# Between the stages of an attention and feed-forward layer: natural token order, first products by column parts, w_out split by halves, evictions and down splits re-dealt

## The chip, the cores and the metric

The kernel runs on one core of a Trainium2 chip. A core has TensorE (PE: matmuls and transposes, with results in PSUM banks), VectorE (DVE), ScalarE (ACT), GpSimd (POOL) and SyncE (SP, which issues the DMAs here). The metric is the device time of one execution in microseconds (us). The granted clock is the share of TensorE's full speed (2.4 GHz) that the chip allowed; the lower of its two levels is 1.2 GHz.

## What is computed

One layer: x is (1024, 1024), float32. Dilated attention in three groups, an output projection w_out (512 to 1024) and a residual; then RMSNorm, an up projection to 2 x 2816, a causal convolution of width 3 over tokens, silu(gate) x up, a down projection and a residual.

```python
def dilated_attention_mixer(h, w_in, q_gain, k_gain, w_out):
    ...
    o = jnp.sum(weights[..., None] * jnp.stack(outs).astype(jnp.float32), axis=0)
    return o.astype(h.dtype).reshape(B, S, ATTN_GROUP_WIDTH) @ w_out

def conv_ffn(h, w_up, conv_w, conv_b, w_down):
    u = causal_depthwise_conv(h @ w_up, conv_w, conv_b)
    gate, up = jnp.split(u, 2, axis=-1)
    return (jax.nn.silu(gate) * up) @ w_down

    ...
        x = x + mix
        x = x + conv_ffn(rms_norm(x, ffn_norm[layer]), ...)
```

## The kernel before, in words

**Products.** A float32 product is three matmuls in fp32r on split operands: a high part h, a cast by ACT, and a low part l = raw - h, a subtract by DVE or POOL. `split` (L514) and `put` (L590) do such a split; the results lie in a ring of 12 buffers (`ring`).

**Stage 1**, to about 604 us, computes the attention in six units over eight token blocks. The last unit runs into what follows.

**Between the stages**, for each of eight token tiles of 128 tokens: `turn_o` (L536) transposes the attention output on PE into a bank otr and splits it (oT), `out_project` (L544) multiplies it with one column half of w_out in 12 matmuls of 512 columns (y) and adds the result to x1, `norm2` (L556) makes the normed tile xn, and `turn2` (L564) transposes that in two halves (xT), which ACT copies to h. The feed-forward products use seven products of quarter operands in place of eight (a Strassen-like scheme over even and odd token tiles and both halves of D): `even` (L594) splits an even tile into the operands b1, `odd` (L598), in three steps, makes the five sums and differences of an odd tile with its even neighbour and splits them into bt. Each pair of tiles fills 128 of the 512 columns of these operands. `split_wo` (L521) splits the four row blocks of w_out, 1024 columns each. The order of the tiles is 0, 1, 2, 3, 4, 6, 5, 7.

**Stage 2** goes over 22 pairs n of a gate and an up feature block. `Pair.first`, `second`, `third` and `fourth` split the weights (wx, wy, wz, wv), `sums` makes the sums that wy and wz are split from (sy, sz), `product(p)` (L664) runs 12 matmuls of 512 columns in the order p = 1, 2, 5, 6, 3, 7, 4 into the banks ua, ub and uc, `evict` (L684) empties a bank on ACT or DVE, and `conv`, `silu`, `gate` and `outer` make the gated rows and their sums, which go to memory.

**Stage 3**, the down projection, has 77 steps (7 products by 11 row blocks). `load_down`, `split_down` and `down` load, split and multiply one step: four token tiles, three matmuls each.

**What sets the order.** The four compute engines run their instructions in the order in which the program calls them. In stage 1 and between the stages that order comes from a list, `plan`: `at(t, f)` puts a call at time t, and the list is sorted by t (N is its length of stage 1, T at L35 has the offsets). From L881 on the calls stand in the order in which they run: the first three pairs by hand, then the loop from L945, then the down steps with LEAD = 2 (how many steps ahead a split stands) and AHEAD = 5 (a load).

```python
    for p, i in enumerate(order):
        t = N + T["t0"] + 6 * p
        at(t + T["to"] if i else t + T["to0"], turn_o, i)
        at(t, out_project, i, 0)
        at(t + 3, out_project, i, 1)
        at(t + 5.8, norm2, i)
```

Of the kernel before, what the change touches and what calls it, by code (L numbers as in the profile page):

```python
# [8 lines left out]
F32 = mybir.dt.float32  # L9
# [26 lines left out]
         sm=6.5, w0=8.3, ws0=9.35, w1=10.0, ws1=11.95, mw=10.0, a0=12.2, a1=13.3, mo=12.2,  # L36
         fin=14.4, t0=4, so0=1.2, so1=1.4, so2=3.2, so3=3.3, to0=-2.2, to=-3.6, n2=3.0, n2s=5.8,
         xf=-9.8, xs=-5.0, xt=-3.5, wp=1, bd=0.5, bh=0)
# [3 lines left out]
def trunk(ctx: ExitStack, tc: tile.TileContext, x, mixer_norm, ffn_norm, w_in, q_gain, k_gain,  # L42
# [477 lines left out]

    def split_wo(kt):  # L521
        M.wo[kt] = split(M.wo[kt], "wo", nc.gpsimd if kt == 1 else nc.vector)

# [12 lines left out]
    def turn_o(i):  # L536
        tr = PA.tile([P, 4, P], F32, name="otr", tag="vp", bufs=1)
        for j in range(4):
            nc.tensor.transpose(tr[:, j], M.ol[i][:, j * P:(j + 1) * P], ident)
        M.oT[i] = oT = ring("oT", [P, 2, 4, P])  # L540
        nc.scalar.copy(oT[:, 0], tr)
        nc.vector.tensor_sub(oT[:, 1], tr, oT[:, 0].bitcast(F32))

    def out_project(i, hf):  # L544
        y = PQ.tile([P, 512], F32, name="y", tag="qk", bufs=2)
        oT = M.oT[i]
        cs = slice(hf * 512, (hf + 1) * 512)
        for kt in range(4):
            wh, wl = M.wo[kt]
            nc.tensor.matmul(y, oT[:, 0, kt], wh[:, cs], start=kt == 0, stop=False)  # L550
            nc.tensor.matmul(y, oT[:, 0, kt], wl[:, cs], start=False, stop=False)
            nc.tensor.matmul(y, oT[:, 1, kt], wh[:, cs], start=False, stop=kt == 3)
        x1 = M.x1[i]
        nc.vector.tensor_add(x1[:, cs], x1[:, cs], y)
# [71 lines left out]
    class Pair:  # L626
# [11 lines left out]

        def first(self):
            self.X = split(self.raw[0], "wx", nc.gpsimd)  # L640

# [10 lines left out]

        def second(self):
            self.Y = split(self.sy, "wy", nc.gpsimd)

        def third(self):
            self.Z = split(self.sz, "wz", nc.gpsimd)

# [4 lines left out]

        def product(self, p):  # L664

# [4 lines left out]
                4: ("V", 0, ("bt", 1), "a", False)}[p]  # L670
            if begin:
                pool, tag, bufs = (M.PL, "b", 2) if bank == "b" or self.n == 0 and bank == "a" else (M.PR, bank, 3)
                self.acc[bank] = pool.tile([P, 512], F32, name="u" + bank, tag=tag, bufs=bufs)
            acc, w, a = self.acc[bank], getattr(self, W), getattr(M, b)
            for k in range(4):
                for n, (z, y) in enumerate(((0, 0), (0, 1), (1, 0))):
                    nc.tensor.matmul(acc, w[z][:, s + k], a[y][:, j, k], start=begin and k == 0 and n == 0,  # L677
                                     stop=k == 3 and n == 2, skip_group_check=True)
            self.evict(p)

# [71 lines left out]

    at(N + 1.05, second_phase)
    at(N + 1.06, make_b1)
    for kt in range(4):
        at(N - 12, load_wo, kt)
        at(N + T[f"so{kt}"], split_wo, kt)
    order = [0, 1, 2, 3, 4, 6, 5, 7]
    for p, i in enumerate(order):
        t = N + T["t0"] + 6 * p  # L760
        at(t - 8 if i < 2 else t - 7, load_o, i)
# [7 lines left out]
        for q in range(2):  # L769
            at(t + 9.2 + .1 * q, turn2, i, q)  # L770
        if i % 2 == 0:
            at(t + 12.2, even, i)
        elif i < 5:
# [106 lines left out]

    p0, p1, p2 = pairs[:3]  # L881
# [24 lines left out]
    p0.product(5)  # L906
    p0.fourth()
    p1.sums(0)
    p0.product(6)
    p1.second()  # L910
    p1.sums(1)
    p0.product(3)
    p0.conv(False)
    p1.third()
    p0.product(7)
    p0.silu()
# [73 lines left out]
    M.RR = M.rr.__enter__()  # L990
    AHEAD, LEAD, TAIL = 5, 2, 3
    acc = {}
    for n, (b, i) in enumerate([(b, i) for b in range(2) for i in range(4)]):
        pool, tag, bufs = (M.PL, "b", 2) if n < 2 else (M.PR, "ac"[n % 2], 3)
        acc[b, i] = pool.tile([P, 512], F32, name="y", tag=tag, bufs=bufs)
    load_down(3)
    load_down(4)
    for m, (p, k) in enumerate(steps):
# [48 lines left out]
```

## Time and profile before

| | |
|---|---|
| median of three runs | 1352.21 us (1351.98 to 1354.04) |
| the profiled execution | 1352.94 us, span 1351.0 us |
| granted clock, mean | 0.981 |
| busy PE / DVE / ACT / POOL | 96% / 67% / 46% / 37% |
| stretches with PE idle or at the lower clock | 603 to 622, 676 to 763, 1127 to 1145 us |

The span is what the profiler saw of the program; the execution's own time has 1.9 us more around it. Times in rows are from the span's start. In a timeline row stand the start, the duration, the engine, the line (L), the operation, out<-in by the program's names and, in brackets, the idle time of that engine before it and what ended it. A matmul's duration includes its drain, which the next one overlaps; the spacing of starts tells the rate.

### The profile page before, as it was taken

How to read it: one execution, taken by the hardware profiler on the slowest of the kernel's cores; microseconds unless marked ns; L12 is line 12 of the kernel's file. 1: busy time of each engine (PE TensorE's matmuls, PEld its weight loads, DVE VectorE, ACT ScalarE, POOL GpSimd, SP SyncE). 2: the span in 40 equal slices, each digit the busy share in tenths (PEclk: the TensorE clock that was granted, in tenths of full speed). 3: DMA queues.
4: the chain of work that ended last, by engine and by line, in shares of the span. 5: the costliest groups of instructions: out<-in, count | busy, mean ns of one | idle time of the engine just before them, and what ended most of it. 6: DMA issues, size and time to landing. Idle time of an engine off the chain costs nothing.

```text
span 1351.0 us, 19176 instructions
## 1 busy us (share of the span) xinstructions
PE 1295.4 (96%) x6887; PEld 1084.4 (80%) x6887; DVE 900.2 (67%) x1537; ACT 615.4 (46%) x1272; POOL 501.2 (37%) x601
## 2 busy tenths in 40 slices
PE   6999999999989999999978899999999998999998
PEld 4898887888878888877766688888888886888887
DVE  4665465554564665556666888888888888776665
ACT  4565354453463453343534445444445445434432
POOL 3333245332364555544544444454445442000000
PEclk9999998999999999997989999999999998999999
DMA  7112211111110211123621323323332328963341
GB/s 238 46 57 76 82 52 56 37 49 58 45 56 25 72 51 36 35 68 113 204 68 39 103 93 112 100 87 92 117 117 87 109 69 306 335 211 107 101 143 60
DMA packets 111613, 132.15 MB, mean 98 GB/s; under 512 B 6126, under 2 KB 80030, under 8 KB 111518
## 3 DMA queue, kind: packets, MB, share of 16 engines
q1 hardware_dynamic: 111518, 130.93, 30.3%
q8 instruction: 54, 0.88, 0.3%
q14 instruction: 41, 0.34, 0.1%
HBM read 95.91 MB, written 35.00 MB: 97 GB/s over the span
## 4 chain that ended last, share of the span: by engine, by line
PE 45%; DVE 3%; POOL 1%; issue 1%; ACT 1%; DMA 0%; DVEq 0%; POOLq 0%; ACTq 0%
PE ua L677 17%; PE y L851 16%; PE uc L677 8%; PE ub L677 4%; DVE c L717 1%; POOL bt L592 0%; DMA graw<-gde 0%; ACT c L715 0%; DVE xn L561 0%; DVE c L728 0%; DVE sy L646 0%; POOL b L592 0%; PE xT L571 0%; ACT xn L559 0%; DVE sz L650 0%
## 5 line engine op out<-in xcount | busy, mean ns | idle before, releaser
L851 PE MATMUL y<-wd,g 128*128 128x512 f32 x924 | 213.3, 393 | 2.7 <-DVE g L592 1.2
L851 PEld LDWEIGHTS y<-wd,g 128*128 128x128 f32 x924 | 175.4, 190 | 40.5 <-DVE g L592 1.5
L198 PE MATMUL qk<-w,hh 128*128 128x512 f32 x384 | 159.4, 415 | 0.0
L199 PE MATMUL qk<-w,hh 128*128 128x512 f32 x384 | 153.8, 401 | 0.0
L200 PE MATMUL qk<-w,hl 128*128 128x512 f32 x384 | 152.6, 397 | 0.5 <-DVE hl L116 0.5
L79 POOL TENSOR_SCALAR ms<-ss 128x8 f32<-128x8 f32 (+1 forms) x64 | 12.8, 201 | 316.2 <-DVE ss L216 265.4
L207 PE MATMUL vp<-w,hh 128*128 128x256 f32 x384 | 122.8, 320 | 3.2 <-DVE v L228 3.1
L717 DVE SCALAR_TENSOR_TENSOR c<-uu,cw,c 128x1023 f32<-128x1023 f32 (+1 forms) x44 | 96.4, 2190 | 39.9 <-ACT c L715 39.2
L209 PE MATMUL vp<-w,hl 128*128 128x256 f32 x384 | 108.8, 283 | 0.0
L208 PE MATMUL vp<-w,hh 128*128 128x256 f32 x384 | 108.8, 283 | 0.0
L518 POOL TENSOR_TENSOR wyl<-sy,wyh 128x1024 fp32r<-128x1024 f32 x22 | 57.9, 2632 | 120.4 <-ACT wyh L517 63.5
L80 POOL TENSOR_TENSOR rs<-ms,half 128x8 f32<-128x8 f32 (+1 forms) x64 | 87.5, 1367 | 5.4
L200 PEld LDWEIGHTS qk<-w,hl 128*128 128x128 f32 x384 | 73.4, 191 | 18.7 <-DVE hl L116 1.2
L207 PEld LDWEIGHTS vp<-w,hh 128*128 128x128 f32 x384 | 73.6, 192 | 18.4 <-DVE v L228 5.6
L314 ACT ACTIVATE sm<-sm,ust 128x128 f32<-128x128 f32 (+1 forms) x128 | 53.3, 418 | 76.0 <-DVE ust L311 73.4
L267 ACT ACTIVATE qT<-tr,gains 128x256 fp32r<-128x256 f32 x48 | 22.7, 473 | 137.8 <-PE tr L256 137.8
L216 DVE TENSOR_REDUCE ss<-qn 128x8 f32<-128x512 f32 x48 | 32.9, 685 | 75.3 <-ACT qn L214 75.3
L208 PEld LDWEIGHTS vp<-w,hh 128*128 128x128 f32 x384 | 73.6, 192 | 9.3
L270 DVE SCALAR_TENSOR_TENSOR qT<-tr,gains,qT 128x256 fp32r<-128x256 f32 x48 | 23.2, 484 | 86.7 <-ACT kT L269 86.7
L198 PEld LDWEIGHTS qk<-w,hh 128*128 128x128 f32 x384 | 74.2, 193 | 0.5 <-ACT hh L115 0.4
L199 PEld LDWEIGHTS qk<-w,hh 128*128 128x128 f32 x384 | 74.3, 194 | 0.1
L311 DVE CUSTOM_DVE_ANT_0 sm<-s,mask 128x128 f32<-128x128 f32 (+1 forms) x192 | 56.1, 348 | 26.4 <-PE s L289 21.0
(182 smaller groups left out, 3374.5 us busy)
## 6 DMA issues: line engine op xcount, KB each, us to landing
uraw<-in_ffn_w_up SPq DMA_DIRECT2D x44, 512.0 KB
raw<-in_attn_w_in SPq DMA_DIRECT2D x48, 384.0 KB
wB<-in_ffn_w_down SPq DMA_DIRECT2D x44, 256.0 KB
graw<-gds SPq DMA_DIRECT2D x44, 256.0 KB
gdo<-c SPq DMA_DIRECT2D x11, 512.0 KB
gds<-gbc SPq DMA_DIRECT2D x11, 512.0 KB
graw<-gdo SPq DMA_DIRECT2D x22, 256.0 KB
ud<-ust SPq DMA_DIRECT2D x32, 132.0 KB
```

The lines of the kernel that those rows point to most:

```text
L80: nc.gpsimd.tensor_tensor(r[:, :n], t[:, :n], half[:, :n], op=ALU.pow)
L198: nc.tensor.matmul(self.qk, a, w[:, 0, :512], start=k == 0, stop=False)
L199: nc.tensor.matmul(self.qk, a, w[:, 1, :512], start=False, stop=False)
L200: nc.tensor.matmul(self.qk, b, w[:, 0, :512], start=False, stop=k == KT - 1)
L207: nc.tensor.matmul(self.vp, a, w[:, 0, 512:], start=k == 0, stop=False)
L208: nc.tensor.matmul(self.vp, a, w[:, 1, 512:], start=False, stop=False)
L209: nc.tensor.matmul(self.vp, b, w[:, 0, 512:], start=False, stop=k == KT - 1)
L311: nc.vector.tensor_tensor_reduce(out=sm[:, h, lo:], in0=src[h], in1=m, op0=ALU.add, op1=ALU.min, scale=-1.0, scalar=3e38, accum_out=st[:, ...
L518: eng.tensor_sub(l, raw, h.bitcast(F32))
L677: nc.tensor.matmul(acc, w[z][:, s + k], a[y][:, j, k], start=begin and k == 0 and n == 0, stop=k == 3 and n == 2, skip_group_check=True)
L717: nc.vector.scalar_tensor_tensor(c[:, k:], u[:, :S - k], cw[:, 2 - k, j:j + 1], c[:, k:], op0=ALU.mult, op1=ALU.add)
L851: nc.tensor.matmul(y, gs[:, z, ts], ws[:, w], start=f and n == 0, stop=k == NK - 1 and n == 2, skip_group_check=True)
```

## The change

1. w_out is split by column halves: `split_wo(kt, hf)` splits 512 columns at a time, the first halves of all four blocks first, the second halves later; `second_phase`, which opens the buffers, comes earlier. `turn_o(0)` comes earlier and uses a bank of tag "s" in place of "vp".
2. Tiles go in the order 0 to 7. Tile 6's operands are split by DVE straight from PSUM, and its copies to h (`turned`) come after that. The steps of `odd(5)` move into the list. Loads and first splits of pairs 0 and 1 come earlier.
3. Products 1 and 2 of pair 0 run on columns 0 to 383 before tile 7 is transposed and on columns 384 to 511 after it. `sum_bank` allocates pair 0's bank uc ahead of pair 1's first bank. wyl and wzl of pair 0 and two bt splits move from POOL to DVE. Sums, conv, gate and outer of pairs 1 to 3 stand at other places.
4. At the end of stage 2 the first three loads stand together, the splits of steps 0, 1 and 2 lie on POOL inside the last pair's products 6, 3 and 7, the first two groups of step 0's matmuls come ahead of the last product 4, and LEAD is 3.

```diff
-         fin=14.4, t0=4, so0=1.2, so1=1.4, so2=3.2, so3=3.3, to0=-2.2, to=-3.6, n2=3.0, n2s=5.8,
+         fin=14.4, t0=4, so=1.2, so0=3.2, so1=3.3, so2=5.1, so3=5.2, to0=-3.43, to=-3.6, n2=3.0, n2s=5.8,
...
-    def split_wo(kt):
-        M.wo[kt] = split(M.wo[kt], "wo", nc.gpsimd if kt == 1 else nc.vector)
+    def split_wo(kt, hf):
+        w = ring("wo", [P, 2, 512])
+        put([w[:, 0], w[:, 1]], M.wo[kt][:, hf * 512:(hf + 1) * 512], nc.gpsimd if kt == 1 else nc.vector)
+        M.wo[kt, hf] = w
...
     def turn_o(i):
-        tr = PA.tile([P, 4, P], F32, name="otr", tag="vp", bufs=1)
+        tag, bufs = ("vp", 1) if i else ("s", 2)
+        tr = PA.tile([P, 4, P], F32, name="otr", tag=tag, bufs=bufs)
...
-        if q == 0 or i % 2 == 0:
-            nc.scalar.copy(M.h[i][:, 4 * q:4 * q + 4], pt)
+        if i < 6 and i % 2 == 0 or i % 2 and q == 0:
+            turned(i, q)
...
     def even(i):
         c = slice(i // 2 * P, (i // 2 + 1) * P)
-        put([b[:, :, :, c] for b in M.b1], M.h[i].rearrange("p (a k) t -> p a k t", a=2), nc.gpsimd)
+        if i < 6:
+            put([b[:, :, :, c] for b in M.b1], M.h[i].rearrange("p (a k) t -> p a k t", a=2), nc.gpsimd)
+        else:
+            for q in range(2):
+                put([b[:, q, :, c] for b in M.b1], M.pt[i, q], nc.vector)
...
-    at(N + 1.05, second_phase)
+    at(N + .56, second_phase)
...
-        at(N + T[f"so{kt}"], split_wo, kt)
-    order = [0, 1, 2, 3, 4, 6, 5, 7]
-    for p, i in enumerate(order):
-        t = N + T["t0"] + 6 * p
+        at(N + T["so"] + .1 * kt, split_wo, kt, 0)
+        at(N + T[f"so{kt}"], split_wo, kt, 1)
+    for i in range(8):
+        t = N + T["t0"] + 6 * i
...
-    at(t - 10, pairs[0].load)
-    at(t - 3, pairs[0].first)
-    at(t + 3, pairs[1].load)
+    at(t - 12, pairs[0].load)
+    at(t - 7.5, pairs[0].first)
+    at(t - 4, pairs[1].load)
+    at(t + 3.1, pairs[1].first)
...
-    odd(5, 0)
-    p1.first()
-    p0.product(1)
-    p0.product(2)
+    p0.product(1, 0, 384)
+    p0.product(2, 0, 384)
     p2.load()
     for q in range(2):
         turn2(7, q)
-    odd(5, 1, nc.vector)
+    p0.product(1, 384)
     odd(7, 0)
+    p0.product(2, 384)
...
-    odd(5, 2, nc.gpsimd)
+    p0.sum_bank()
+    odd(7, 1, onV)
     p1.product(1)
+    odd(7, 2, onV)
     p2.first()
     p1.product(2)
     p0.sums(0)
-    p0.second()
-    odd(7, 1, nc.vector)
+    p0.second(onV)
     p2.product(1)
-    odd(7, 2, nc.gpsimd)
     p0.sums(1)
     p2.product(2)
-    p0.third()
+    p0.third(onV)
...
+        if p is None:
+            for m in range(8):
+                b, i = divmod(m, 4)
+                pool, tag, bufs = (M.PL, "b", 2) if m < 2 else (M.PR, "ac"[m % 2], 3)
+                if m == 2:
+                    down(0, 0)
+                    down(0, 1)
+                    old.product(4)
+                acc[b, i] = pool.tile([P, 512], F32, name="y", tag=tag, bufs=bufs)
+            old.conv(True)
+            old.gate()
+            break
         old.product(4)
         old.conv(True)
-        if p is None:
-            split_down(1, nc.gpsimd)
-            old.gate()
-            break
...
-            split_down(0, nc.gpsimd)
-            load_down(2)
+            split_down(0, onG)
         p.product(3)
...
+            split_down(1, onG)
         p.product(7)
+        if not new:
+            split_down(2, onG)
...
-    AHEAD, LEAD, TAIL = 5, 2, 3
+    AHEAD, LEAD, TAIL = 5, 3, 3
```

**ACT at the end of stage 1**, around the first splits of w_out (woh and wo are the high parts of w_out, oT the split attention output, v and pT belong to stage 1). Before:

```order
L214 ACTIVATE qn<-qk 128x512
L227 CAST v<-vp 128x4x64
L517 CAST woh<-wraw 128x1024
L328 CAST pT<-pt 128x512
L517 CAST woh<-wraw 128x1024
L541 CAST oT<-otr 128x512
L364 ACTIVATE e<-e 128x12
L517 CAST woh<-wraw 128x1024 x2
L328 CAST pT<-pt 128x512
```

Now:

```order
L214 ACTIVATE qn<-qk 128x512
L544 CAST oT<-otr 128x512
L227 CAST v<-vp 128x4x64
L597 CAST wo<-wraw 128x512 x2
L328 CAST pT<-pt 128x512
L597 CAST wo<-wraw 128x512 x2
L364 ACTIVATE e<-e 128x12
L597 CAST wo<-wraw 128x512 x2
L328 CAST pT<-pt 128x512
```

The cast of the first oT stands ahead of v, and the first halves of w_out are cast 512 columns at a time, two to a place, where one of 1024 stood.

**DVE at the start of stage 2** (h and bt are `odd`'s, ug the evictions of product 2, sy and sz the sums of the weights, wyl and wzl low parts of pair 0). Before:

```order
L692 TENSOR_TENSOR ug<-p_7697,ub 128x4x128
L592 TENSOR_TENSOR bt_7254<-h,bt_7253 128x8x128
L604 TENSOR_TENSOR h<-xT,h 128x512
L605 TENSOR_TENSOR h<-xT,h 128x512
L606 TENSOR_TENSOR h<-xT,h 128x512
L592 TENSOR_TENSOR bt_7254<-xT,bt_7253 128x4x128
L608 TENSOR_TENSOR h<-h 128x512
L692 TENSOR_TENSOR ug<-p_7757,ub 128x4x128
L646 TENSOR_TENSOR sy<-uraw 128x512
L647 TENSOR_TENSOR sy<-sy,uraw 128x512
```

Now:

```order
L598 TENSOR_TENSOR bt_7262<-xT,bt_7261 128x4x128
L618 TENSOR_TENSOR h<-h 128x512
L707 TENSOR_TENSOR ug<-p_7752,ub 128x4x128
L598 TENSOR_TENSOR bt_7262<-h,bt_7261 128x8x128 x2
L707 TENSOR_TENSOR ug<-p_7794,ub 128x4x128
L656 TENSOR_TENSOR sy<-uraw 128x512
L657 TENSOR_TENSOR sy<-sy,uraw 128x512
L518 TENSOR_TENSOR wyl<-sy,wyh 128x1024
L660 TENSOR_TENSOR sz<-uraw,sy 128x512
L661 TENSOR_TENSOR sz<-uraw 128x512
L707 TENSOR_TENSOR ug<-p_7837,ub 128x4x128
L518 TENSOR_TENSOR wzl<-sz,wzh 128x1024
```

Two splits into bt follow one another, and the splits wyl and wzl stand among the evictions and the sums; before, they were POOL's.

**ACT at the end of stage 2** (wd and g are a down step's operands, u and uu evictions of the last pair, c its conv and silu). Before:

```order
L591 CAST wv<-uraw 128x512
L698 COPY u_10697<-ua 128x512
L591 CAST wd<-wB_10657 128x512
L591 CAST g<-graw 128x512
L715 ACTIVATE c<-ug,cw 128x1024
L725 ACTIVATE c<-c 128x1024
L706 COPY uu<-ua 128x4x128
L715 ACTIVATE c<-uu,cw 128x1024
L591 CAST wd<-wB_10681 128x512
```

Now:

```order
L597 CAST wv<-uraw 128x512
L713 COPY u_10735<-ua 128x512
L597 CAST wd<-wB_10691 128x512
L597 CAST g<-graw 128x512
L597 CAST wd<-wB_10695 128x512
L597 CAST g<-graw 128x512
L597 CAST wd<-wB_10699 128x512
L597 CAST g<-graw 128x512
L730 ACTIVATE c<-ug,cw 128x1024
L740 ACTIVATE c<-c 128x1024
L721 COPY uu<-ua 128x4x128
L730 ACTIVATE c<-uu,cw 128x1024
```

Three steps are cast ahead of the conv of the gate half, where one was; the second step stood behind the conv of the up half.

## Rows read from the trace of the kernel before

**Rows 1.** The page, part 1: busy us (share of the span) and instructions of TensorE:

```profile
PE 1295.4 (96%) x6887; PEld 1084.4 (80%) x6887; DVE 900.2 (67%) x1537; ACT 615.4 (46%) x1272; POOL 501.2 (37%) x601
```

**Rows 2.** Windows view of three stretches; the line ahead of them names the columns:

```profile
core 0: us, PE busy (x) PEld busy (x) DVE busy (x) ACT busy (x) POOL busy (x), PEclk, DMA share, GB/s
603.00:622.00 19.00, 15.77 (x66) 11.56 (x65) 12.76 (x23) 8.81 (x18) 9.32 (x13) 0.64 0.29 103
676.00:763.00 87.00, 71.90 (x283) 54.98 (x283) 60.94 (x54) 34.34 (x43) 38.18 (x18) 0.92 0.20 61
1127.00:1145.00 18.00, 14.41 (x47) 10.50 (x46) 14.24 (x17) 10.19 (x18) 1.81 (x1) 0.81 1.00 361
```

**Rows 3.** Timeline of PE, 604 to 624 us: start, duration, instruction, idle before it:

```profile
605.52 0.66 PE L539 MATMUL otr<-ident,ol 128*128 128x128 f32 x4 [1.72 <-DVE v L228]
...
607.58 0.50 PE L550 MATMUL y<-woh,oT 128*128 128x512 f32 x1 [0.97 <-ACT oT L541]
...
612.08 0.80 PE L551 MATMUL y<-wol,oT 128*128 128x512 f32 x1 [0.53 <-DVE wol L518]
```

**Rows 4.** The same timeline: spacing of 512-column matmuls at both clock levels:

```profile
613.10 0.63 PE L550 MATMUL y<-woh,oT 128*128 128x512 f32 x1
613.53 0.68 PE L551 MATMUL y<-wol,oT 128*128 128x512 f32 x1
...
623.60 0.39 PE L550 MATMUL y<-woh,oT 128*128 128x512 f32 x1
623.82 0.39 PE L551 MATMUL y<-wol,oT 128*128 128x512 f32 x1
```

**Rows 5.** Groups by line of PE, 676 to 763 us: busy and mean, then idle before and its releasers:

```profile
L677 PE MATMUL ua<-b,wxh 128*128 128x512 f32 x32 | 13.1, 499 | 3.4 <-DVE h L604 3.4
L677 PE MATMUL ua<-bt,wv 128*128 128x512 f32 x36 | 10.6, 450 | 4.8 <-DVE uu L704 4.8
...
L677 PE MATMUL ua<-b,wxl 128*128 128x512 f32 x16 | 8.0, 500 | 1.9 <-POOL wxl L518 1.9
L677 PE MATMUL uc<-bt,wyh 128*128 128x512 f32 x24 | 7.8, 400 | 0.4 <-DVE bt L592 0.4
...
L677 PE MATMUL uc<-bt,wyl 128*128 128x512 f32 x12 | 5.0, 412 | 1.4 <-POOL wyl L518 1.4
L677 PE MATMUL uc<-bt,wzl 128*128 128x512 f32 x12 | 4.8, 404 | 0.9 <-POOL wzl L518 0.9
...
L571 PE MATMUL xT<-ident,xn 128*128 128x128 f32 x16 | 2.1, 276 | 2.4 <-DVE xn L561 2.4
```

**Rows 6.** Timelines of ACT and DVE, 604 to 616 us: splits of w_out:

```profile
604.58 1.04 ACT L517 CAST woh<-wraw 128x1024 fp32r<-128x1024 f32 x1
...
610.73 2.63 DVE L518 TENSOR_TENSOR wol<-wraw,woh 128x1024 fp32r<-128x1024 f32 x2 [0.61 <-ACT woh L517]
```

**Rows 7.** Timelines of DVE and POOL, 666 to 730 us: one instruction beside POOL and before it:

```profile
668.55 1.28 DVE L561 SCALAR_TENSOR_TENSOR xn<-x,rs,gbc 128x1024 f32<-128x1024 f32 x1 [2.17 <-POOL rs L80]
...
675.38 3.38 DVE L561 SCALAR_TENSOR_TENSOR xn<-x,rs,gbc 128x1024 f32<-128x1024 f32 x1 [3.76 <-POOL rs L80]
...
675.32 2.37 POOL L592 TENSOR_TENSOR b<-h,b 128x1024 fp32r<-128x1024 f32 x1
```

**Rows 8.** Groups by line of PE, 1127 to 1145 us:

```profile
L851 PE MATMUL y<-wd,g 128*128 128x512 f32 x32 | 11.1, 505 | 2.7 <-DVE g L592 1.2 <-POOL wd L592 0.9 <-ACT g L591 0.6
L677 PE MATMUL ua<-bt,wv 128*128 128x512 f32 x12 | 3.1, 405 | 0.8 <-DVE uu L704 0.8
```

**Rows 9.** Timeline of ACT, 1120 to 1142 us:

```profile
1125.80 1.24 ACT L715 ACTIVATE c<-ug,cw 128x1024 f32<-128x1024 f32 x1 [2.14 <-DVE ug L700]
...
1133.72 0.60 ACT L591 CAST wd<-wB 128x512 fp32r<-128x512 f32 x1
```

**Rows 10.** Timeline of PE, 595 to 597 us: matmuls of 128 and of 64 columns:

```profile
595.95 0.31 PE L340 MATMUL u<-v,pT 128*128 128x128 f32 x1
596.09 0.24 PE L342 MATMUL u<-v,pT 128*128 128x64 f32 x1
```

More of the change, by code (lines that the diff above doesn't have):

```diff
@@ L548, in out_project @@
         for kt in range(4):
[L549 to L552, printed above, removed]
+            w = M.wo[kt, hf]
+            nc.tensor.matmul(y, oT[:, 0, kt], w[:, 0], start=kt == 0, stop=False)
+            nc.tensor.matmul(y, oT[:, 0, kt], w[:, 1], start=False, stop=False)
+            nc.tensor.matmul(y, oT[:, 1, kt], w[:, 0], start=False, stop=kt == 3)
         x1 = M.x1[i]
@@ L571, in turn2, with turned @@
             nc.tensor.transpose(pt[:, j], M.n2[i][:, kt * P:(kt + 1) * P], ident)
-        if q == 0 or i % 2 == 0:
-            nc.scalar.copy(M.h[i][:, 4 * q:4 * q + 4], pt)
+        if i < 6 and i % 2 == 0 or i % 2 and q == 0:
+            turned(i, q)
+    def turned(i, q):
+        nc.scalar.copy(M.h[i][:, 4 * q:4 * q + 4], M.pt[i, q])
     def make_b1():
@@ L637, in load, with first @@
                 self.raw.append(r)
-        def first(self):
-            self.X = split(self.raw[0], "wx", nc.gpsimd)
+        def first(self, eng=nc.gpsimd):
+            self.X = split(self.raw[0], "wx", eng)
         def sums(self, step):
@@ L651, in sums, with second, third @@
                 nc.vector.tensor_sub(s[:, 4:], g[:, :4], r[:, :4])
[L653 to L657, printed above, removed]
+        def second(self, eng=nc.gpsimd):
+            self.Y = split(self.sy, "wy", eng)
+        def third(self, eng=nc.gpsimd):
+            self.Z = split(self.sz, "wz", eng)
         def fourth(self):
@@ L662, in fourth, with product @@
             self.V = v[:, 0], v[:, 1]
-        def product(self, p):
+        def product(self, p, lo=0, hi=512):
             W, s, (b, j), bank, begin = {
@@ L670, in product @@
                 4: ("V", 0, ("bt", 1), "a", False)}[p]
-            if begin:
+            if begin and lo == 0 and bank not in self.acc:
                 pool, tag, bufs = (M.PL, "b", 2) if bank == "b" or self.n == 0 and bank == "a" else (M.PR, bank, 3)
@@ L676, in product, with sum_bank @@
                 for n, (z, y) in enumerate(((0, 0), (0, 1), (1, 0))):
-                    nc.tensor.matmul(acc, w[z][:, s + k], a[y][:, j, k], start=begin and k == 0 and n == 0,
-                                     stop=k == 3 and n == 2, skip_group_check=True)
-            self.evict(p)
+                    nc.tensor.matmul(acc[:, lo:hi], w[z][:, s + k], a[y][:, j, k, lo:hi],
+                                     start=begin and lo == 0 and k == 0 and n == 0, stop=k == 3 and n == 2,
+                                     skip_group_check=True)
+            if hi == 512:
+                self.evict(p)
+        def sum_bank(self):
+            self.acc["c"] = M.PR.tile([P, 512], F32, name="uc", tag="c", bufs=3)
         def part(self, name):
@@ L770, in trunk @@
             at(t + 9.2 + .1 * q, turn2, i, q)
-        if i % 2 == 0:
+        if i == 6:
+            at(t + 9.4, even, i)
+            at(t + 12, turned, i, 0)
+            at(t + 12.1, turned, i, 1)
+        elif i % 2 == 0:
             at(t + 12.2, even, i)
-        elif i < 5:
+        else:
             at(t + 9.35, odd, i, 0)
@@ L878, in sum_up @@
             nc.sync.dma_start(out[quadrant(a, i)], X[a, i])
-    p0, p1, p2 = pairs[:3]
-    odd(5, 0)
-    p1.first()
-    p0.product(1)
-    p0.product(2)
+    p0, p1, p2, p3 = pairs[:4]
+    onV, onG = nc.vector, nc.gpsimd
+    p0.product(1, 0, 384)
+    p0.product(2, 0, 384)
     p2.load()
@@ L910, in trunk @@
     p1.second()
+    p0.product(3)
     p1.sums(1)
-    p0.product(3)
+    p0.product(7)
     p0.conv(False)
     p1.third()
-    p0.product(7)
     p0.silu()
@@ L920, in trunk @@
     p0.conv(True)
-    pairs[3].load()
     p1.product(6)
     p2.sums(0)
+    p1.product(3)
+    p2.second()
     p0.gate()
-    p2.second()
-    p1.product(3)
-    p2.sums(1)
+    p3.load()
     p1.product(7)
     p1.conv(False)
+    p2.sums(1)
     p2.third()
@@ L936, in trunk @@
     p2.product(6)
-    pairs[3].first()
+    p3.first()
+    p2.product(3)
+    p3.sums(0)
     p1.gate()
-    p1.outer(0)
-    p2.product(3)
-    pairs[3].sums(0)
     p2.product(7)
     p2.conv(False)
-    pairs[3].sums(1)
+    p3.sums(1)
+    p1.outer(0)
+    acc = {}
     for n in range(3, NF + 1):
@@ L965, in trunk @@
             M.RL = M.rl.__enter__()
-            load_down(0)
+            for m in range(3):
+                load_down(m)
         p.product(5)
@@ L970, in trunk @@
         p.fourth()
-        if not new:
-            load_down(1)
         p.product(6)
@@ L981, in trunk @@
             new.sums(0)
+        else:
+            split_down(1, onG)
         p.product(7)
+        if not new:
+            split_down(2, onG)
         p.conv(False)
@@ L990, in trunk @@
     M.RR = M.rr.__enter__()
-    AHEAD, LEAD, TAIL = 5, 2, 3
[L992 to L995, printed above, removed]
+    AHEAD, LEAD, TAIL = 5, 3, 3
     load_down(3)
@@ L1011, in trunk @@
             for i in range(4):
-                down(m, i)
+                if m or i > 1:
+                    down(m, i)
     for i in range(4):
```

2 lines of the change are left out of this document (1 added, 1 removed).

## The prediction

> **What bounds the kernel now.** I read the page's busy shares first: TensorE (PE) is busy 1295.4 us of the 1351.0 us span [rows 1], so PE sets the time and every other engine matters only where PE waits for it. Then the windows view, where the reader is to see three stretches in which PE stands idle or runs at the lower of its two clock levels: 603 to 622 us, where the attention stage ends and the out projection begins, 676 to 763, where the first feed-forward pairs begin, and 1127 to 1145, where the down projection begins [rows 2]. Each has two losses. The idle time comes from the timeline and the groups of lines: 1.0 + 0.5 + 1.7 = 3.2 us in the first [rows 3]; 3.4 + 4.8 + 1.9 + 0.4 + 1.4 + 0.9 + 2.4 = 15.2 in the second [rows 5]; 2.7 + 0.8 = 3.5 in the third [rows 8]. The clock's loss comes from the granted clock of the windows. A granted clock of 0.64 over 19 us is (1 - 0.64) / 0.5 x 19 = 13.7 us at 1.2 instead of 2.4 GHz; 0.92 over 87 us is 13.9; 0.81 over 18 us is 6.8 [rows 2]. A 512-column matmul follows the last after 0.43 us at the lower level and 0.22 at the full one [rows 4], so work at the lower level loses about half its time. With some of those spells idle, I take 6.5, 6.2 and 3.2 us lost. In all 9.7 + 21.4 + 6.7 = 37.8 us can be attacked; the rest of the span has nothing that this change touches.
>
> **First junction (w_out halves, otr in another bank).** The first transposes (otr) wait 1.72 us for a VectorE (DVE) instruction, v, only because both use one PSUM bank; the change gives them another bank, so that wait goes, and the 0.97 us for their cast shrinks with it [rows 3]. The first product y waits again at 612.08 for wol and ends at about 614.4 (two spacings of 0.43 after 613.53) [rows 3, 4]. Before it needs four casts of 1024 columns on ScalarE (ACT), 4 x 1.04 = 4.2 us, three subtracts on DVE (two of them 2.63 together) and one on GpSimd (POOL) [rows 6]. The change needs half the columns for this product: an estimate of 4 x 0.60 = 2.4 us on ACT, by the 512-column cast of [rows 9], and 3 x 0.66 on DVE, half of a 1024-column subtract each. The first product would then end at 610.2 at full clock or 611.8 at the lower one, by laying those durations end to end on each queue. The second halves add four casts and four subtracts later: 8 x 0.60 - 4 x 1.04 = 0.6 us more on ACT in total, hidden since ACT is busy 8.81 of the 19 us [rows 2]. From 614.4 to the end of tile 0's second product at 624.28 is 9.9 us [rows 4], most of it at the lower clock. If the spell shortens, the gain is the first product's 2.6 to 4.2 us plus up to 2.2 of clock; if it stays whole, the second product ends at some 622.7, 1.5 us earlier than now. So the gain lies between 1.5 and 6.4 us. I take 3.5, nearer to the end where the lower clock persists for half its stretch, because the clock fell here after PE had waited 1.72 and 0.97 us, and the change takes away the first of these and not all of the second.
>
> **Second junction (natural order, column parts, re-dealt evictions).** What goes: the 3.4 us wait of pair 1's first product on the DVE subtract h [rows 5]. It exists because its bank is that of the last xT; with the sum bank allocated first, that bank falls to product 5, which comes much later. What shrinks: the 2.4 us before xT. The norm xn in front of it took 3.38 us where a POOL subtract b had just begun, against 1.28 for the same instruction when DVE was first [rows 7]; tiles 6 and 7 now come last, the even tile's operands are read from PSUM, and POOL has less there. I lay the new order out with the durations of the trace and find these waits: 1.5 before xT of tile 6, 0.8 before the second column part's operands, 1.5 before xT of tile 7, 1.6 for pair 2's wxl (1.9 in all now), 1.7 + 2.0 for pair 2's product 5 behind the conv chain on DVE, which takes the place of the 4.8 us for uu, and 1.6 in four small ones: together 10.7 against 15.2. So 4.5 us of waiting goes. Of the clock's 6.2, one spell of 1.75 is taken to stay. The column split turns 24 matmuls of 512 columns into 24 of 384 and 24 of 128. A 128-column matmul with its weight load takes 0.14 us to the next [rows 10], and 384 columns by three quarters of the 512-column spacing [rows 4] 0.165; so 24 x (0.165 + 0.14 - 0.22) = 2.0 us at most, nothing at least (equal columns), and I take 1.0. By the Trainium skill, "TensorE: Matmul & The Clock Gate", section "Back-to-back issue gap", the isolated spacing is columns / 2.4 ns plus 2.5 ns, which would make the split cost 24 x 2.5 ns = 0.06 us; the row of 0.14 speaks against it at 128 columns, and the sum doesn't rest on it. The gain here is 4.5 + 6.2 - 1.75 - 1.0 = 8.0 us, between 3 (two more spells stay) and 11 (no spell, no split cost). Of the moved loads on SP's queue, pair 0's and pair 1's go earlier; DMA is busy 0.20 of this window [rows 2], so I cost them at nothing. If that cover were gone, p1's first split would come late and PE would wait as it now does for wxl, 1.9 us.
>
> **Third junction (splits of steps 0 to 2 on POOL, two down groups ahead of product 4).** Now the second step's cast wd starts only at 1133.72, behind the conv, whose first instruction on ACT starts at 1125.80 [rows 9]. That is why PE waits for wd and g, 2.7 us, and runs at the lower clock [rows 2, 8]. The change puts six casts of 0.60 us ahead of the conv on ACT. Two of them stand there already, so 4 x 0.60 = 2.4 us come on top, and ACT idles 2.14 us before the conv's first instruction [rows 9]; that instruction starts up to 0.5 us later. Steps 1 and 2 are then ready by 1127. Product 4 waits 0.8 us for uu [rows 8]; the two down groups, 6 x 0.22 = 1.3 us, lie in that gap. What is late next is step 3, whose splits still stand behind the conv: by my layout 0.4 to 0.7 us of waiting. The gain is 3.5 - 0.6 + 3.2 = 6.1, taken as 6.0; at worst 3 (the clock's part stays), at best 6.7.
>
> **Sum.** 3.5 + 8.0 + 6.0 = 17.5 us. Against the profiled execution's own 1352.94 us this gives 1335.4. The median of the runs is 0.73 below that execution, so I forecast **1334.7 us**. The ends add up to gains of 7.5 and 24.1 us, 1344.7 and 1328.1 us.
>
> **Rivals.** *A: the waits only move.* The first product ends sooner but the lower clock lasts whole in the first junction (1.5), the DVE chain from the evictions through conv is late in the second (3), and the third keeps half its spell (4.5). That gives 9.0 us, 1343.2. For it speaks that DVE is busy 60.94 of 87 us [rows 2] and takes on more; against it, that three waits go by construction. *B: no change.* The second junction pays back what it gained, since pair 3's operands come no earlier out of the same POOL and DVE queues, and the other two move inside the noise: about 1352. POOL's 38.18 of 87 us [rows 2] speaks against it. *C: slower.* The change moves pair 0's wyl and wzl and a bt split to DVE, all with two SBUF inputs, while POOL splits wxl, wyl and wzl of pairs 1 and 2. Where the two met, xn took 3.38 instead of 1.28 us, a price of 2.1 us [rows 7]. The mechanism decides from 9 such meetings on PE's path (9 x 2.1 = 18.9 > 17.5); with 12 it gives +25.2 - 17.5 = 7.7 us, 1359.9. The Trainium skill, "SBUF — State Buffer", section "Who interferes with whom", says that a DVE instruction with two SBUF inputs and a POOL instruction that reads SBUF exclude each other for the whole instruction; by that rule, the trace agrees, at 3.38 against 1.28 us. Against C: about four splits, some 10 us, leave POOL in the same stretch, and only a few of DVE's additions stand on PE's path.
>
> **How the numbers follow.** The forecast gets 0.70, A 0.17, B 0.05, C 0.08. About 0.2% or 2.7 us is what a measurement of this kernel can tell from no change. The forecast and A are faster by more than that, 0.87; B is the same, 0.05; C is slower, 0.08. The range takes in the forecast's ends and A's: 1326 to 1347 us, a little wider than the sums since my layout of the second junction is by hand.
>
> **What would show it.** Right: the granted clock between 603 and 622 rises from 0.64, no wait over 1 us before otr and none of 3 us before pair 1's first product, a gap of at most 0.8 us after the first six down matmuls, and a granted clock near 1 in the tail. Wrong: DVE instructions on wyl or wzl of 2.5 us or more with POOL busy beside them (C); the same times at the tail's start and the pair loop's entry, with idle time grown elsewhere (B); a clock still at the lower level through the first product (A). The steady pairs between and the down steps must keep their durations; if they change, the sum is wrong in a part I did not cost.

## The result and the profile after

The changed kernel takes 1336.43 us (median of four runs, 1336.1 to 1338.69) against 1352.1 (1349.5 to 1354.04): a ratio of 0.9889, 95% interval 0.9869 to 0.9909, or 15.7 us less. The forecast was 1334.7, the range 1326 to 1347. Between the two profiled executions the spans differ by 1351.0 - 1334.2 = 16.8 us; the sum had said 17.5.

To place the gain I cut both timelines at four marks: the last projection of values in stage 1, the first product of tile 1, product 4 of pair 3, and one spacing (0.23 us) behind the last matmul of the last pair's product 7. These are rows of PE's timeline at the marks, before the change:

```profile
603.52 0.29 PE L209 MATMUL vp<-w,hl 128*128 128x256 f32 x1
...
625.07 0.48 PE L550 MATMUL y<-woh,oT 128*128 128x512 f32 x1
...
779.54 1.79 PE L677 MATMUL ua<-bt,wv 128*128 128x512 f32 x7
...
1127.21 0.40 PE L677 MATMUL ua<-bt,wzl 128*128 128x512 f32 x1
```

And of the timeline after it, where the last mark is the first row of the down projection:

```profile
603.64 0.28 PE L209 MATMUL vp<-w,hl 128*128 128x256 f32 x1
...
621.25 0.47 PE L553 MATMUL y<-wo,oT 128*128 128x512 f32 x1
...
769.16 2.03 PE L687 MATMUL ua<-bt,wv 128*128 128x512 f32 x8
...
1117.06 1.54 PE L871 MATMUL y<-wd,g 128*128 128x512 f32 x6
```

The differences of these starts make the table. Idle is the length of a stretch less PE's busy time in it by the windows view (in the third, over its first 25 us); lower clock is the time at 1.2 GHz, 2 x (1 - granted clock) x length by the same view, in the second stretch added up over windows of 6 us, because the view rounds the clock to a hundredth.

| stretch | before: us, idle, lower clock | after: us, idle, lower clock | forecast, measured gain |
|---|---|---|---|
| first junction | 21.55, 3.2, 13.8 | 17.61, 3.1, 3.5 | 3.5, 3.9 |
| second, to pair 3's product 4 | 154.47, 16.6, 13.6 | 147.91, 13.5, 3.4 | 8.0, 6.6 |
| pairs 3 to 21 | 347.90 | 347.90 | 0, 0 |
| third, to the end | 223.56, 3.6, 7 | 217.14, 0.2, 0 | 6.0, 6.4 |

Stage 1 ends 0.1 us later. **Most of the gain is clock, not idle time**: idle falls by 6.6 us in all and narrow matmuls cost 1.3, so that some 11 of the 16.9 us are left for the clock; the time at the lower level falls by some 27 us. PE's busy time on the page says the same: 1295.4 us before [rows 1], 1284.2 after, with 24 matmuls more. In the windows view, over the corresponding stretches, the granted clock stands at 0.91, 0.98 and 1.00, where [rows 2] had 0.64, 0.92 and 0.81:

```profile
core 0: us, PE busy (x) PEld busy (x) DVE busy (x) ACT busy (x) POOL busy (x), PEclk, DMA share, GB/s
603.00:621.00 18.00, 15.00 (x82) 11.04 (x80) 13.88 (x30) 10.98 (x31) 8.87 (x14) 0.91 0.34 116
668.00:755.00 87.00, 77.57 (x351) 62.38 (x352) 61.76 (x64) 39.42 (x51) 30.82 (x16) 0.98 0.20 59
1117.00:1135.00 18.00, 17.76 (x77) 14.01 (x76) 14.59 (x19) 10.64 (x18) 0.58 (x1) 1.00 1.01 358
```

In the first junction the timeline of PE shows otr without a wait, where [rows 3] had 1.72 us. The first product waits three times for w_out instead, 2.30 us together, and its last matmuls still start 0.43 us apart; it ends at 612.0, against 614.4:

```profile
603.76 0.60 PE L542 MATMUL otr<-ident,ol 128*128 128x128 f32 x4
...
605.85 0.50 PE L553 MATMUL y<-wo,oT 128*128 128x512 f32 x1 [1.05 <-ACT wo L597]
606.85 0.50 PE L554 MATMUL y<-wo,oT 128*128 128x512 f32 x1 [0.50 <-DVE wo L598]
...
608.56 0.60 PE L554 MATMUL y<-wo,oT 128*128 128x512 f32 x1 [0.75 <-POOL wo L598]
...
611.10 0.63 PE L554 MATMUL y<-wo,oT 128*128 128x512 f32 x1
611.53 0.63 PE L555 MATMUL y<-wo,oT 128*128 128x512 f32 x1
```

In the second, the groups of PE answer to [rows 5]: the 3.4 us for h and the 4.8 for uu are gone, wxl stands nearly as it was, pair 2's product 5 waits 1.3 + 2.1, and the transposes xT now wait 5.4 us in place of 2.4:

```profile
L687 PE MATMUL ua<-b,wxh 128*128 128x512 f32 (+2 forms) x40 | 11.2, 364 | 0.0
L687 PE MATMUL ub<-b,wxh 128*128 128x512 f32 (+2 forms) x40 | 11.0, 359 | 0.7 <-DVE x L557 0.7
L687 PE MATMUL ua<-bt,wv 128*128 128x512 f32 x36 | 9.1, 403 | 0.0
L687 PE MATMUL uc<-bt,wyh 128*128 128x512 f32 x26 | 9.1, 434 | 1.3 <-ACT wyh L517 1.3
...
L687 PE MATMUL ua<-b,wxl 128*128 128x512 f32 (+2 forms) x20 | 7.3, 363 | 1.8 <-POOL wxl L518 1.8
...
L687 PE MATMUL uc<-bt,wyl 128*128 128x512 f32 x13 | 5.9, 451 | 2.1 <-POOL wyl L518 2.1
...
L574 PE MATMUL xT<-ident,xn 128*128 128x128 f32 x24 | 3.2, 277 | 5.4 <-DVE xn L564 5.4
```

In the third, the group of [rows 8] had 2.7 us of waiting, and the timeline now shows none:

```profile
1117.06 1.54 PE L871 MATMUL y<-wd,g 128*128 128x512 f32 x6
1118.44 2.96 PE L687 MATMUL ua<-bt,wv 128*128 128x512 f32 x12
1121.24 4.04 PE L871 MATMUL y<-wd,g 128*128 128x512 f32 x17
```

A little is left further on, too short for a bracket of its own in PE's timeline: in the windows view PE is busy 9.76 of the 10 us from 1127 on, and the timeline of the weight loads (PEld) shows what they waited for, the low parts of step 3 on DVE:

```profile
1127.00:1137.00 10.00, 9.76 (x42) 7.54 (x41) 9.96 (x16) 5.56 (x11) 0.00 (x0) 1.00 1.03 364
```

```profile
1128.59 0.19 PEld L871 LDWEIGHTS y<-wd,g 128*128 128x128 f32 x1 [0.56 <-DVE wd L598]
1129.19 1.92 PEld L871 LDWEIGHTS y<-wd,g 128*128 128x128 f32 x9 [0.42 <-DVE g L598]
```

### The profile page after: what moved, and what is told of

It is laid out like the page before. It is cut to its first block, busy times and chain, and to the rows that moved or that the text cites. A ratio compares the mean times of both kernels' runs of the same rounds, so it can differ in the third digit from the quotient of the medians.

```text
span 1334.2 us, 19243 instructions
## 1 busy us (share of the span) xinstructions
PE 1284.2 (96%) x6911; PEld 1078.4 (81%) x6911; DVE 901.2 (68%) x1544; ACT 616.0 (46%) x1277; POOL 495.9 (37%) x599
## 4 chain that ended last, share of the span: by engine, by line
PE 43%; DVE 3%; issue 2%; DMA 1%; POOL 1%; ACT 1%; SPq 0%; DVEq 0%; POOLq 0%; ACTq 0%
PE ua L687 15%; PE y L871 15%; PE uc L687 8%; PE ub L687 4%; DVE c L732 1%; DMA wB<-in_ffn_w_down 1%; POOL wxl L518 0%; DMA graw<-gde 0%; ACT c L730 0%; DVE sz L660 0%; DVE sy L656 0%; DVE c L743 0%; DVE bt L598 0%; POOL wyl L518 0%; POOL wzl L518 0%
## 5 line engine op out<-in xcount | busy, mean ns | idle before, releaser
L871 PE MATMUL y<-wd,g 128*128 128x512 f32 x924 | 210.4, 389 | 0.2
L518 POOL TENSOR_TENSOR wxl<-uraw,wxh 128x1024 fp32r<-128x1024 f32 x22 | 58.4, 2653 | 44.8 <-ACT wxh L517 44.7
```

Source lines behind the costliest of these rows:

```text
L518: eng.tensor_sub(l, raw, h.bitcast(F32))
L871: nc.tensor.matmul(y, gs[:, z, ts], ws[:, w], start=f and n == 0, stop=k == NK - 1 and n == 2, skip_group_check=True)
```

## The experiments

My theory was the forecast's: each part of the change removes the wait that the trace names. Rivals were that one part of each junction carries it all, and C, that DVE is the worse place for the splits. Each undo is cut at the same marks, so that only its own stretch speaks. Not undone one by one were the order of the tiles, tile 6's split from PSUM and the earlier loads and first splits.

**The bank of otr.**

```diff
-to0=-3.43
+to0=-2.2
-        tag, bufs = ("vp", 1) if i else ("s", 2)
+        tag, bufs = "vp", 1
```

> The change with one part undone: the first transposes (otr) use the bank of tag vp again, at their old place. If the bank matters by itself, the wait of 1.7 us for v returns, the first product y ends about 2 us later than the change's 612.0, and the time is 1.7 to 3.8 us above the change's 1336.4: 1338.1 to 1340.2. Rival, that the halves of w_out carry the whole gain of this junction: the first product still waits for the low parts of w_out, and the time is within 0.5 us of 1336.4.

1337.93 us (1336.21 to 1339.11). First junction 19.05 us in place of 17.61, idle 3.4 in place of 3.1: the 1.73 us before otr is back, and the first product then waits for its cast but no longer for w_out. The idle time moves by 0.3 us; the rest of the 1.44 is a spell of 6.9 us in place of 3.5. So the bank alone is worth little idle time, and the rival is nearer; the four times overlap with those of the change.

**The halves of w_out.**

```diff
-so=1.2, so0=3.2, so1=3.3, so2=5.1, so3=5.2
+so0=1.2, so1=1.4, so2=3.2, so3=3.3
...
-    def split_wo(kt, hf):
...
+    def split_wo(kt):
...
-        at(N + T["so"] + .1 * kt, split_wo, kt, 0)
-        at(N + T[f"so{kt}"], split_wo, kt, 1)
+        at(N + T[f"so{kt}"], split_wo, kt)
```

> The change with one part undone: w_out is split 1024 columns at a time again, at the old places; the otr bank stays changed. If the halves matter, the first product ends 2.0 to 4.2 us later than 612.0 and the time is 1338.4 to 1340.2. Rival, that the 1.7 us wait before otr set off the long spell at the lower clock: the spell between 603 and 622 us stays as short as in the change (some 3.5 us) and the time is within 1 us of 1336.4.

The casts go back to their old places with this edit. 1342.12 us (1340.99 to 1342.92). First junction 23.40 us, 5.8 more than with halves and 1.9 more than before the change. PE is idle 1.3 us longer in all, and 16.8 us run at the lower clock. The timeline shows the waits for a cast and for the low parts of 1024 columns:

```profile
606.49 0.50 PE L551 MATMUL y<-woh,oT 128*128 128x512 f32 x1 [1.48 <-ACT woh L517]
607.75 0.50 PE L552 MATMUL y<-wol,oT 128*128 128x512 f32 x1 [0.76 <-DVE wol L518]
...
610.35 0.79 PE L552 MATMUL y<-wol,oT 128*128 128x512 f32 x1 [1.63 <-POOL wol L518]
...
612.89 0.80 PE L552 MATMUL y<-wol,oT 128*128 128x512 f32 x1 [0.53 <-DVE wol L518]
```

All four times lie above those of the change, so the halves, with the places of their casts, carry this junction. The rival (the wait before otr set off the long spell) falls: without that wait this profile has a spell as long as before.

**The two down groups ahead of product 4.**

```diff
                 if m == 2:
-                    down(0, 0)
-                    down(0, 1)
                     old.product(4)
+                    down(0, 0)
+                    down(0, 1)
```

> The change with one part undone: the first two groups of step 0's matmuls stand behind the last product 4 again. If they cover the wait for uu, PE waits 0.8 us ahead of product 4 and the time is 0.8 to 1.5 us above 1336.4: 1337.2 to 1337.9. Rival, that the earlier splits alone carry the third junction and product 4 waits for nothing: 1336.4.

1336.46 us (1334.63 to 1339.16). In its profile the third junction is 0.34 us longer; PE waits 0.85 us for uu, as before the change. The wait is as told, its price less than half of it: 0.24 us come back at step 3, whose wait is gone in this profile, and where the rest comes back stays open.

**The early splits of steps 1 and 2.**

```diff
-            split_down(1, onG)
...
-            split_down(2, onG)
...
             old.conv(True)
+            split_down(1, onG)
-    AHEAD, LEAD, TAIL = 5, 3, 3
+    AHEAD, LEAD, TAIL = 5, 2, 3
```

> The change with one part undone: only step 0 is split inside the last pair, step 1 behind the conv and step 2 with LEAD 2, as before; the two groups ahead of product 4 stay. If the splits carry the junction, PE waits 2 to 3 us in the first steps, the lower clock returns there, and the time is 4.5 to 6.3 us above 1336.4: 1340.9 to 1342.7. Rival, that the two groups ahead of product 4 give the splits enough room: at most 1 us above.

1340.62 us (1340.36 to 1343.05). Third junction 222.39 us, 5.25 of the 6.42 gained. The groups of PE have the releasers of [rows 8] again:

```profile
L871 PE MATMUL y<-wd,g 128*128 128x512 f32 x39 | 11.7, 447 | 3.8 <-ACT g L597 1.7 <-DVE g L598 1.2 <-POOL wd L598 0.9
```

**The sum bank.** One line less:

```diff
-    p0.sum_bank()
```

> The change with one part undone: the sum bank of pair 0 is not allocated ahead, so that pair 1's first product takes the bank that the last xT is read from. If that bank made the 3.4 us wait of before, PE waits 2.5 to 3.5 us for the DVE subtracts of tile 7 ahead of pair 1's first product, a spell at the lower clock may follow, and the time is 2.5 to 5 us above the change's 1336.4: 1338.9 to 1341.4. Rival, that the narrow products behind the last xT give DVE the time: within 0.7 us of 1336.4.

1338.91 us (1338.71 to 1340.25). Second junction 2.8 us longer: PE waits 0.97 us for bt ahead of pair 1's first product, and 3 us more run at the lower clock. The wait is there, at a third of the 3.4 us it had before the change, and the narrow products now stand between xT and it, as the rival said.

**Where the splits of pair 0 run.**

```diff
-    odd(7, 2, onV)
+    odd(7, 2, onG)
-    p0.second(onV)
+    p0.second()
-    p0.third(onV)
+    p0.third()
```

> The change with one part undone: pair 0's wyl and wzl and the last split of tile 7 into bt go to POOL again. If DVE was the better place, PE waits again for low parts in product 5 or 3 of pair 0 (0.4 to 2 us) and the time is 0.5 to 4 us above 1336.4. Rival, that VectorE's splits collide with GpSimd's and cost more than they give: the time is 1 us or more below 1336.4.

1339.74 us (1337.55 to 1340.43). Tile 5's two splits stay as the change has them. Second junction 3.3 us longer, idle 15.2 in place of 13.5; the rest is a spell more at the lower clock. The wait comes through POOL's queue: pair 2's wxl stands behind the bt split there, and PE waits 3.55 us for it in place of 1.79:

```profile
693.62 2.41 POOL L598 TENSOR_TENSOR bt<-h,bt 128x1024 fp32r<-128x1024 f32 x1 [9.63 <-ACT bt L597]
695.98 2.79 POOL L518 TENSOR_TENSOR wxl<-uraw,wxh 128x1024 fp32r<-128x1024 f32 x1
```

```profile
698.83 0.80 PE L687 MATMUL ua<-b,wxl 128*128 128x512 f32 x1 [3.55 <-POOL wxl L518]
```

So VectorE is the better place by the 1.8 us that this wait grows, and rival C falls. C's own sign, splits of wyl or wzl of 2.5 us or more on DVE, had not come in the change either:

```profile
698.03 1.23 DVE L518 TENSOR_TENSOR wyl<-sy,wyh 128x1024 fp32r<-128x1024 f32 x1 [1.11 <-ACT wyh L517]
...
701.68 1.22 DVE L518 TENSOR_TENSOR wzl<-sz,wzh 128x1024 fp32r<-128x1024 f32 x1
```

**The column parts.**

```diff
-    p0.product(1, 0, 384)
-    p0.product(2, 0, 384)
...
-    p0.product(1, 384)
+    p0.product(1)
     odd(7, 0)
-    p0.product(2, 384)
+    p0.product(2)
```

> The change with one part undone: products 1 and 2 of pair 0 run whole behind the transposes of tile 7. Without the column parts PE has nothing to run while it waits for xn of tile 7: the wait there, 1.6 us now, grows by the 384-column work of some 4.2 us, less the 1.3 us that narrow matmuls cost, and the time is 3 to 6 us above 1336.4 (a spell at the lower clock included). Rival, that work behind waits less in exchange: within 1 us of 1336.4.

1342.18 us (1340.08 to 1344.37). Second junction 154.58 us, 6.7 more. Before the change it took 154.47: natural order without the column parts gains nothing there in this profile. Idle is 17.9 us in place of 13.5, and 17 us run at the lower clock in place of 3.4, some of it behind other waits than the one of 6.71 us for xn of tile 7:

```profile
682.81 1.94 PE L574 MATMUL xT<-ident,xn 128*128 128x128 f32 x8 [6.71 <-DVE xn L564]
```

**The changed kernel again**, since the undo runs showed the first junction at 17.6 or 19.9 us for the same instructions.

> The changed kernel again, nothing edited. The stretch from the last projection of values (603.6 us) to tile 1's first product took 17.6 us in most of the profiles so far and 19.9 in two, for the same instructions. If the length of the spell at the lower clock there differs from one execution to the next, this profile has one of the two lengths again, the other stretches repeat within 0.3 us, and the times lie between 1334 and 1340 with 1336 the likeliest. Rival, that the two long ones come from the edits that those kernels have elsewhere: 17.6 us again.

1336.85 us (1335.81 to 1339.66). The first junction took 17.36 us, so the expectation missed the place but not the matter: this profile, of the run of 1339.66, lost its time in the second junction, 152.88 us against 147.91. The large waits are the same, idle is even 1.3 us less. After the same wait for xn of tile 5 the matmuls start 0.43 us apart here, and 0.23 in the first profile, whose row follows:

```profile
667.27 1.78 PE L574 MATMUL xT<-ident,xn 128*128 128x128 f32 x8 [2.71 <-DVE xn L564]
...
669.28 0.63 PE L554 MATMUL y<-wo,oT 128*128 128x512 f32 x1
669.70 0.63 PE L555 MATMUL y<-wo,oT 128*128 128x512 f32 x1
```

```profile
668.58 1.09 PE L574 MATMUL xT<-ident,xn 128*128 128x128 f32 x8 [2.72 <-DVE xn L564]
...
670.22 0.40 PE L553 MATMUL y<-wo,oT 128*128 128x512 f32 x1
670.45 0.39 PE L554 MATMUL y<-wo,oT 128*128 128x512 f32 x1
```

The windows view of this execution has a granted clock of 0.85 from 660 to 690 us; the first had 1.00:

```profile
660.00:690.00 30.00, 25.23 (x123) 21.80 (x123) 21.92 (x25) 13.76 (x22) 13.78 (x10) 0.85 0.43 131
```

```profile
660.00:690.00 30.00, 23.87 (x135) 20.12 (x134) 22.30 (x25) 14.77 (x24) 14.60 (x11) 1.00 0.48 146
```

So after a wait of this length the clock fell in one execution and not in another. The spell parts of the undo prices above have this uncertainty, up to 5 us; the idle parts repeat within 1.5. All times of the undos of the halves, of the early splits and of the column parts lie above the eight of the changed kernel (1335.81 to 1339.66). Those of the other four undos overlap with them, so that there only the waits and the idle time speak.

**Three edits at the longest waits left** (f1): tile 4's split on DVE, pair 2's cast earlier, pair 2's sums ahead of pair 0's conv.

```diff
-            at(t + 12.2, even, i)
+            at(t + (11.85 if i == 4 else 12.2), even, i)
...
-M.h[i].rearrange("p (a k) t -> p a k t", a=2), nc.gpsimd)
+M.h[i].rearrange("p (a k) t -> p a k t", a=2), nc.vector if i == 4 else nc.gpsimd)
...
     p0.sum_bank()
+    p2.first()
...
+    p2.sums(0)
     p0.conv(True)
     p1.product(6)
-    p2.sums(0)
+    p2.second()
     p1.product(3)
-    p2.second()
```

> The change and three edits at its longest waits between 660 and 735 us: the split of tile 4 goes to DVE ahead of the norm of tile 5 (now 3.37 us beside POOL), pair 2's first cast stands two calls earlier, and pair 2's sums stand ahead of the conv of pair 0's up half. If these waits (2.7, 1.8, 1.3 and 2.1 us) end as the trace names them, 4 to 7 us go: 1329.4 to 1332.4. Rival, that the next instruction in the same queue is late in turn: within 1.5 us of 1336.4.

1330.59 us (1330.03 to 1332.5). Second junction 143.42 us, 4.5 less than in the first profile: idle falls by 3.7 us and no part runs at the lower clock. xn of tile 5 takes 1.28 us, where the change had this beside POOL (DVE's row, then POOL's):

```profile
665.16 3.37 DVE L564 SCALAR_TENSOR_TENSOR xn<-x,rs,gbc 128x1024 f32<-128x1024 f32 x1 [2.61 <-POOL rs L80]
```

```profile
665.09 2.36 POOL L598 TENSOR_TENSOR b<-h,b 128x1024 fp32r<-128x1024 f32 x1
```

**The first junction again, and a split moved back** (f2, on f1).

```diff
-so=1.2
+so=.575
...
-nc.gpsimd if kt == 1 else nc.vector
+nc.gpsimd if kt == 3 else nc.vector
...
-            at(t + 14.7, odd, i, 2, nc.vector)
+            at(t + (15.5 if i == 5 else 14.7), odd, i, 2, nc.vector)
```

> The kernel f1 and two more edits: the first halves of w_out are cast ahead of pT, with the fourth instead of the second low part on POOL, and DVE's last split of tile 5 into bt stands behind the residual adds of tile 7 and the splits of tile 6. If PE's waits name their causes, the first product waits 0.5 to 1.3 us less for w_out (its first wait stays), and the waits for xn of tile 7 and for the add ahead of ub (1.6 and 0.7) lose 1 to 2 us together: 1327.0 to 1329.0 with a spell in the first junction as in f1, 2.3 less without. Rival, that the split that was moved behind is late in turn or meets POOL's wxl there: within 0.7 us of f1's 1330.6.

1333.36 us (1328.12 to 1334.21). The first junction takes 15.35 us without a spell, better than expected; the second 148.06, worse: PE waits 2.47 us for xn of tile 7 and a spell follows. The two waits of f1 there, 1.59 and 0.68 us, became one. The split that was moved takes 2.87 us on DVE beside POOL's wxl, as the rival said, and xn of tile 7 comes no sooner for it. It cost more than the rival said through the spell, 10 us at the lower clock; one of the four runs, 1328.12, has the time of f3 below.

**The first edit of f2 alone** (f3), and **two moves around the norm of tile 7** (f4, on f3):

```diff
-            at(t + 14.7, odd, i, 2, nc.vector)
+            at(t + (17.85 if i == 5 else 14.7), odd, i, 2, nc.vector)
...
-    at(t + 3.1, pairs[1].first)
+    at(t + 5.9, pairs[1].first)
```

> The kernel f1 with the edit on the halves of w_out of f2 alone; tile 5's split stands where f1 has it. If f2 lost its gain to that split (PE waited 2.47 us for xn of tile 7 there, and a spell at the lower clock followed), the first junction takes 15.4 us as in f2, the stretch from the last product y to pair 3's product 4 takes 91 us as in f1, and the time is 1327.5 to 1329.0. Rival, that f2's long stretch was only a spell of that one execution: 1330 to 1333 again in some of the runs, with the same waits as f1.

> The kernel f3 and two moves: pair 1's first split stands behind the norm of tile 7, so that GpSimd is free for that norm's scale, and tile 5's last split stands behind the norm as well. If GpSimd's wxl and the split were what kept xn of tile 7 late, PE's waits of 1.6 and 0.7 us there lose 1.5 us or more and the time is 1.5 to 2.3 us below f3's. Rival, that pair 1's wxl is now late for its first product: a wait of 1 us or more there and no gain over f3.

f3: 1328.55 us (1328.41 to 1329.3), first junction 15.35, second 143.41, as the theory had it; no run shows the 1330 us or more of the rival. f4: **1326.98 us** (1326.83 to 1328.33), ratio to before the change 0.9825, 95% interval 0.9812 to 0.9839, beyond the change's own and 1.6 us below f3, at the lower end of what was expected. Its second junction takes 142.09: the waits of 1.6 and 0.7 us are gone, one of 0.94 for ug ahead of pair 1's product 2 is new. Both junctions run at full clock:

```profile
602.00:618.00 16.00, 13.93 (x84) 10.09 (x83) 13.41 (x30) 11.36 (x30) 10.45 (x14) 1.00 0.38 124
664.00:745.00 81.00, 75.22 (x344) 59.64 (x342) 61.74 (x62) 38.80 (x51) 31.99 (x16) 1.00 0.22 67
```

## Why the prediction was right

**First junction, 3.5 forecast, 3.9 measured.** The size was right, its make-up not. I had the bank's wait go and the first product wait less. The bank's 1.72 us went, but waits for w_out of 0.50 and 0.75 us took much of its place, and idle time fell by 0.2 us only. The product's end came as forecast for the lower clock, 612.0 against 611.8. What shortened was the spell, 13.8 to 3.5 us; with whole columns it was 16.8. Rival A's case (the spell stays whole) was no case of the change but of some executions: in two profiles of kernels with these very instructions (u2_pool and f1) the junction took 19.84 and 19.87 us, a gain of 1.7. That the size fits so well is luck in part.

**Second junction, 8.0 forecast, 6.6 measured.** Idle time was the mis-sized term: I had 4.5 us less, the table has 3.1. The waits for wxl (1.6 forecast, 1.79) and for product 5 of pair 2 (1.7 + 2.0, against 1.32 + 2.13) were right, and those for tiles 6 and 7 nearly (1.5 each, against 1.12 and 1.59). The 0.8 us came as 0.71, but ahead of product 2's first column part and for a residual add; of the 1.6 in four small waits 0.2 came in that window. What I missed is 2.72 us for xn of tile 5. The meeting of xn with POOL's split b [rows 7] did not go with the new order: the norm of tile 5 met the split of tile 6 before, and it meets that of tile 4 now. f1 shows its price: with that split on DVE the wait was 0.64 us. The step that failed is the sentence that POOL has less there: it had less behind tile 6, not at tile 5. Pair 0's first split, which the change moved ahead, moved along: on POOL its wxl stands right before the small instructions of that norm in both traces (from 672.04 us for 2.40 before, from 661.52 for 2.70 now); whether that makes the meeting was not tried. The clock's part, 6.2 less 1.75 for one spell, came out: 3.4 us at the lower clock were left of 13.6.

The column split cost 24 x (0.173 + 0.113 - 0.23) = 1.3 us, against the 1.0 taken. The spacings are three 384-column matmuls from 681.30 to 681.82, and three of 128 columns from 686.28 to 686.62:

```profile
681.30 0.51 PE L687 MATMUL ub<-b,wxh 128*128 128x384 f32 x2
...
681.82 0.51 PE L687 MATMUL ub<-b,wxh 128*128 128x384 f32 x2
...
686.28 0.38 PE L687 MATMUL ub<-b,wxh 128*128 128x128 f32 x2
...
686.62 0.39 PE L687 MATMUL ub<-b,wxh 128*128 128x128 f32 x2
```

By the Trainium skill, "TensorE: Matmul & The Clock Gate", section "Back-to-back issue gap", it would have cost an estimated 0.06 us; its spacing for an isolated 128-column matmul is about 56 ns, which the section itself calls too low for narrow matmuls with weight loads between, and the rows have 113. The measurement decides.

**Third junction, 6.0 forecast, 6.4 measured.** The splits are 5.25 of it by their undo, as the sum had them. The wait at step 3, behind the conv, came as told but smaller: 0.24 us in place of 0.4 to 0.7. The two down groups cover the 0.85 us that they were said to cover, and are worth 0.34.

**Rival C** was wrong in its direction: putting the splits back on POOL cost 3.3 us in its stretch, 1.8 of them waiting. Of the splits into bt, two moved to DVE, and one, tile 5's first, went the other way, to POOL. Meetings of DVE with POOL were there (xn of tile 5 at 3.37 us above all), but the idle time of the stretch fell by 3.1 us with them, and the nine that C needed on PE's path would have added 18.9. B had a false premise, since pairs 3 to 21 took 347.90 us in both kernels and handed nothing back.

## What to carry to other kernels

Cut both timelines at the same marks and keep idle time and the time at the lower clock apart: here 6.6 us of waiting less came with some 11 us through the clock, and the idle part repeats better from run to run. When an order is changed, look for a meeting of two engines at its new place before counting it as gone. A reordering may be worth nothing alone; here it needed work for PE in the gap, the column parts.

## What the runs showed of the hardware that I had not expected

The same instructions after the same wait kept the full clock in one execution and lost it in another: 2.72 us of waiting was followed by 0.23 us spacings, 2.71 us by 0.43, and the first junction had 3.5 us at the lower clock in most profiles and 13.5 in two. The spread of the times goes with it: 3.9 us in eight runs of the changed kernel, 0.9 in four of f3 and 1.5 in five of f4, whose junctions have no wait over 1.61 and 1.19 us; the kernel before, run on the same chip as f3 and f4, spread by 4.1 in nine. Which condition decides between the two was not tried.
